# Mixer steps cut into pieces and placed between projections: a two-layer trunk on one core

## The chip, the core and the metric

One core of a Trainium2 chip runs the whole program. The metric is device microseconds of one execution, as the median of several runs. TensorE (PE) multiplies, VectorE (DVE) and ScalarE (ACT) work elementwise, GpSimd (POOL) does small elementwise work, SyncE (SP) issues the loads. Matrix products write PSUM, eight banks per partition, of which the kernel gives four to its pool a (projections), three to pool b (small steps) and one to sums.

## What is computed

Two layers, each a half-step SwiGLU feed-forward, four token mixers side by side with one input and one output projection, and a second feed-forward; 256 tokens, width 1024, everything in float32. Each section is normed and modulated by a conditioning vector.

```python
for l in range(DEPTH):
    cond = (c_act @ ada_w[l] + ada_b[l])[:, None, :]
    sh1, sc1, g1, sh2, sc2, g2, sh3, sc3, g3 = jnp.split(cond, N_MOD, axis=-1)
    h = modulate(rmsnorm(x, norm_g[l, 0]), sh1, sc1)
    x = x + 0.5 * g1 * swiglu(h, ffn1_w13[l], ffn1_w2[l])
    h = modulate(rmsnorm(x, norm_g[l, 1]), sh2, sc2)
    x = x + g2 * hybrid_mixer(h, ...)   # forgetting attention | mLSTM | retention | SSD, @ w_in before, @ w_out behind
    h = modulate(rmsnorm(x, norm_g[l, 2]), sh3, sc3)
    x = x + 0.5 * g3 * swiglu(h, ffn2_w13[l], ffn2_w2[l])
return rmsnorm(x, final_g)
```

In the mixers, the columns rq, rk (retention) are rotated, sx, sbc (SSD) and mq, mk (mLSTM) go through a causal convolution of four taps and a SiLU, mv, fv, rv are values, sz, mo, rg are gates, fq, fk are queries and keys of the forgetting attention.

## The kernel before

Activations lie feature by token (128 features by 256 tokens, eight tiles). Every float32 product is three products of a rounded type: each weight tile of 512 KB is loaded by SP into one of four buffers (raw), ACT rounds it (whi, L204), DVE subtracts (wlo, L205), and PE multiplies high by high, high by low and low by high (L222 to L224, or L767 to L769 for projections that come out token by feature). split() and wload() do this for all weights.

The conditioning vector is worked out beside everything else: each of its 128 rows that are not needed at the start is a 512 KB load (araw) and one multiply-and-sum on DVE (L263). Calls of background() in the feed-forward columns, the blocks of W2 and the projections start as many as the table BG says for the stage, in pairs (calls, sums); flush() makes up what a section needs.

A section's norm is put off: pre_begin and pre_tile scale the residual by the gain alone (uh, ul, with two extra columns for the shift), square it on ACT and add the squares on POOL (acc, L343). The first projections of a section run on these columns while the sum is finished: mm_two calls stat_end after six of eight feature tiles (L351 on PE, rs on ACT L372, a power on POOL L373), and later rows() (L378 on PE), which gives R, the row of norms. What was multiplied raw is then scaled by R and shifted. norm_h() makes the normed columns hh, hl for the rest (L407, L411, L412).

mixers_in walks through the list ORDER. A name with "p." projects (project), the others are steps that consume a projection or earlier steps; here every step is traced in one go. rq and rk are projected raw (proj_first), scaled in first_evac from PSUM; the others use h. Four PSUM banks hold projections. Steps use banks of pool b. Steps of the mixers proper: ssd (tables, scores, values), ret, mlstm, fox and foxb (softmax attention, front and back); ssdb, mo, rg, foxb make the four outputs y, which go through PE transposes and put_y into yh, yl. turns keeps outputs whose transposes are put off into W_out. W_out runs in two passes over all eight column tiles, with the outputs of fox and mLSTM first, then SSD and retention, holding the half-sums of eight tiles in four banks; in the second pass each tile is added to the residual (resid, L426) and taken up by pre_tile for the next section.

The order in which each engine gets its instructions is not the traced one. A scheduler takes instructions by a priority, which is the traced order (raised by HP within high_priority), as its own estimates say that their operands are ready; keep_in_program_order holds an instruction to its place on its engine. Each engine then takes its queue in order.

## Time and profile before

| | us |
|---|---|
| median of 3 runs | 1089.21 (1088.49 to 1089.78) |
| profiled execution, its own time | 1086.47 |
| its span, first to last instruction | 1084.7 |
| PE busy | 1055.8 (97%) |
| DVE busy | 856.0 (79%) |
| ACT busy | 535.9 (49%) |
| POOL busy | 68.8 (6%) |
| mean granted clock of PE | 0.993 |

The page counts an engine as busy while an instruction of it runs; products overlap on PE, so 283 ns is the time of one product from start to end, and one starts about every 0.12 us. Layer 0's mixers lie from 208 to 360 us, layer 1's from 740 to 884. The chain of work that ended last is PE for 76% of the span.

### The profile page before, as it was taken

How to read it: one execution, taken by the hardware profiler on the slowest of the kernel's cores; microseconds unless marked ns; L12 is line 12 of the kernel's file. 1: busy time of each engine (PE TensorE's matmuls, PEld its weight loads, DVE VectorE, ACT ScalarE, POOL GpSimd, SP SyncE). 2: the span in 40 equal slices, each digit the busy share in tenths (PEclk: the TensorE clock that was granted, in tenths of full speed). 3: DMA queues.
4: the chain of work that ended last, by engine and by line, in shares of the span. 5: the costliest groups of instructions: out<-in, count | busy, mean ns of one | idle time of the engine just before them, and what ended most of it. 6: DMA issues, size and time to landing. Idle time of an engine off the chain costs nothing.

```text
span 1084.7 us, 21679 instructions
## 1 busy us (share of the span) xinstructions
PE 1055.8 (97%) x8725; PEld 1039.9 (96%) x8725; DVE 856.0 (79%) x1505; ACT 535.9 (49%) x890; POOL 68.8 (6%) x87
## 2 busy tenths in 40 slices
PE   8999999889999999999999999999999999999997
PEld 6999999889899999999999999999999999999997
DVE  6899788879866999887679988767997689876551
ACT  4565434455445845434464543445545566554451
POOL 0000001200011300000100000012001130000010
PEclk9999999989999999999999999999999999999999
DMA  9889889947444679888657988865654366865541
GB/s 368 332 309 347 298 296 322 317 171 226 144 134 137 214 256 345 302 289 304 215 214 244 352 278 316 286 213 193 191 179 137 116 213 209 298 213 184 187 137 39
DMA packets 74022, 258.29 MB, mean 238 GB/s; under 512 B 10177, under 2 KB 12609, under 8 KB 73410
## 3 DMA queue, kind: packets, MB, share of 16 engines
q1 hardware_dynamic: 73634, 256.39, 68.5%
q8 instruction: 68, 1.11, 0.4%
q10 hardware_dynamic: 288, 0.52, 0.1%
q14 instruction: 32, 0.26, 0.1%
HBM read 255.83 MB, written 1.05 MB: 237 GB/s over the span
## 4 chain that ended last, share of the span: by engine, by line
PE 76%; DVE 8%; DMA 8%; issue 3%; ACT 3%; POOL 1%; SPq 0%; POOLq 0%; DVEq 0%; ACTq 0%
PE pa L222 22%; PE pa L223 22%; PE pa L224 22%; DMA araw<-in_ada_dram 3%; DVE wlo L205 2%; PE pa L769 2%; PE pa L767 2%; PE pa L768 1%; ACT whi L204 1%; DMA raw<-in_w2a_dram 1%; DVE araw L263 1%; PE pb L820 1%; DMA raw<-in_wfm_dram 1%; DVE ul L400 1%; DMA sh<-in_ada_dram 1%
## 5 line engine op out<-in xcount | busy, mean ns | idle before, releaser
L204 ACT ACTIVATE whi<-raw 128x1024 fp32r<-128x1024 f32 (+1 forms) x340 | 354.5, 1047 | 275.3 <-PE pa L223 79.4
L205 DVE TENSOR_TENSOR wlo<-raw,whi 128x1024 fp32r<-128x1024 f32 (+1 forms) x340 | 409.6, 1212 | 87.5 <-ACT whi L204 79.4
L222 PE MATMUL pa<-hh,whi 128*128 128x256 f32 x1424 | 403.2, 283 | 1.7 <-ACT whi L204 1.1
L223 PE MATMUL pa<-hl,whi 128*128 128x256 f32 x1424 | 403.4, 283 | 0.0
L224 PE MATMUL pa<-hh,wlo 128*128 128x256 f32 x1424 | 402.3, 283 | 0.5 <-DVE wlo L205 0.5
L222 PEld LDWEIGHTS pa<-hh,whi 128*128 128x128 f32 x1424 | 273.5, 192 | 3.6 <-ACT whi L204 2.3
L224 PEld LDWEIGHTS pa<-hh,wlo 128*128 128x128 f32 x1424 | 271.3, 191 | 1.2 <-DVE wlo L205 0.7
L223 PEld LDWEIGHTS pa<-hl,whi 128*128 128x128 f32 x1424 | 271.3, 191 | 0.5 <-issue 0.5
L263 DVE CUSTOM_DVE_ANT_0 araw<-araw,cact 128x1024 f32<-128x1024 f32 x128 | 158.1, 1235 | 48.1 <-DMA araw<-in_ada_dram 47.5
L224 PE MATMUL pa<-sh,wlo 128*128 128x256 f32 x660 | 184.3, 279 | 0.0
L222 PE MATMUL pa<-sh,whi 128*128 128x256 f32 x660 | 184.3, 279 | 0.0
L223 PE MATMUL pa<-sl,whi 128*128 128x256 f32 x660 | 184.3, 279 | 0.0
L222 PEld LDWEIGHTS pa<-sh,whi 128*128 128x128 f32 x660 | 125.1, 190 | 0.0
L224 PEld LDWEIGHTS pa<-sh,wlo 128*128 128x128 f32 x660 | 125.1, 190 | 0.0
L223 PEld LDWEIGHTS pa<-sl,whi 128*128 128x128 f32 x660 | 125.1, 189 | 0.0
L539 ACT ACTIVATE sh<-s 128x256 fp32r<-128x256 f32 x88 | 36.1, 411 | 116.0 <-DVE s L532 108.7
L343 POOL TENSOR_TENSOR acc<-acc,sq 128x256 f32<-128x256 f32 x40 | 35.8, 894 | 697.6 <-ACT sq L338 696.7
L223 PE MATMUL pa<-ul,whi 128*128 128x258 f32 x208 | 60.6, 291 | 2.5 <-DVE ul L400 2.5
L222 PE MATMUL pa<-uh,whi 128*128 128x258 f32 x208 | 61.2, 294 | 0.0
L767 PE MATMUL pa<-whi,hh 128*128 128x256 f32 (+1 forms) x192 | 57.0, 298 | 3.1 <-ACT hh L411 3.1
L224 PE MATMUL pa<-uh,wlo 128*128 128x258 f32 x208 | 60.0, 289 | 0.0
L769 PE MATMUL pa<-whi,hl 128*128 128x256 f32 (+1 forms) x192 | 56.0, 295 | 0.0
(276 smaller groups left out, 1379.6 us busy)
## 6 DMA issues: line engine op xcount, KB each, us to landing
araw<-in_ada_dram SPq DMA_DIRECT2D x128, 512.0 KB, 5.7
raw<-in_w13b_dram SPq DMA_DIRECT2D x88, 512.0 KB, 5.1
raw<-in_w13a_dram SPq DMA_DIRECT2D x76, 512.0 KB, 5.7
raw<-in_w2a_dram SPq DMA_DIRECT2D x44, 512.0 KB, 5.5
raw<-in_w2b_dram SPq DMA_DIRECT2D x44, 512.0 KB, 4.6
raw<-in_wfm_dram SPq DMA_DIRECT2D x32, 512.0 KB, 5.0
raw<-in_wtm_dram SPq DMA_DIRECT2D x24, 512.0 KB, 4.1
raw<-in_wo_dram SPq DMA_DIRECT2D x16, 512.0 KB, 4.7
```

Source lines behind the costliest of these rows:

```text
L204: act.activation(out=hi, in_=raw, func=AF.Copy)
L205: dve.tensor_tensor(out=lo, in0=raw, in1=hi.bitcast(F32), op=ALU.subtract)
L222: pe.matmul(o, lhsT=wh, rhs=xh, start=first, stop=False, **kw)
L223: pe.matmul(o, lhsT=wh, rhs=xl, start=False, stop=False, **kw)
L224: pe.matmul(o, lhsT=wl, rhs=xh, start=False, stop=last, **kw)
L263: dve.tensor_tensor_reduce(out=raw, in0=raw, in1=cact, scale=0.5, scalar=0.0, op0=ALU.mult, op1=ALU.add, accum_out=cond[l][:, i:i + 1])
L343: eng.tensor_tensor(out=s.acc, in0=s.acc, in1=sq, op=ALU.add)
L400: dve.scalar_tensor_tensor(out=s.ul[:, k, :T], in0=xT[:, k, :], scalar=s.G[:, k:k + 1], in1=s.uh[:, k, :T].bitcast(F32), op0=ALU.mult, op1 ...
L539: act.activation(out=sh[:, c, :], in_=s, func=AF.Copy)
L767: pe.matmul(os[t], lhsT=h[0][:, k, ts], rhs=wh[:, y, :], start=(k == 0), stop=False)
L768: pe.matmul(os[t], lhsT=h[0][:, k, ts], rhs=wl[:, y, :], start=False, stop=False)
L769: pe.matmul(os[t], lhsT=h[1][:, k, ts], rhs=wh[:, y, :], start=False, stop=(k == KT - 1))
```

## The change

- ORDER is written anew, and steps may be generators: a step runs to its next yield each time its name stands in ORDER (step()), so that a step's pieces lie between projections. There are nine yields per layer: two in ssd, one in ret, three in mlstm, two in fox (which takes in foxb), one in ssdb.
- sx is projected raw too, behind rq and rk. Raw projections are copied from PSUM by ACT (two copies each), and scaled by R later (rqe, rke, sxe).
- The convolutions of sbc, mq and mk read a copy in SBUF that ACT makes (copied) instead of PSUM.
- All POOL instructions are held in program order. The clearing of kz and bz becomes a step (clear) behind h; h is traced at high priority.
- The per-layer row of gate and norm parameters (row) is loaded in the first feed-forward of the layer.
- W_out takes six column tiles in two passes (SSD and retention first, then fox and mLSTM) in three banks, and the last two tiles in one pass each; the last piece of fox and the two put-off outputs lie among the first pass. The weights are laid out to match.
- BG: layer 0's first feed-forward starts 35 sums instead of 40, with 4 instead of 6 in its last three calls; layer 0's mixers 13 instead of 8, all in the last six projections; in the two feed-forwards between, more in the columns and fewer in W2.
- Two of the first four products of a feed-forward's raw columns go to banks of pool b. acc and R have one buffer instead of two.

```diff
-WO_GROUPS = ((0, 1), (3, 2))
-WO_TURNS = 2, 5
-WO_TILES = (0, 2, 4, 6, 1, 3, 5, 7)
+WO_GROUPS = ((3, 2), (0, 1))
+NP = 6
...
-BG = [((16, 15), (5, 13), (6, 12)), ((8, 0), (5, 8)), ((14, 14), (6, 0), (10, 18)), ((14, 14), (6, 0), (10, 18)),
-      ((8, 0), (5, 8)), ((14, 8),)]
+BG = [((16, 17), (1, 0), (7, 14), (3, 4)), ((8, 0), (6, 13)), ((2, 0), (13, 18), (5, 0), (10, 14)), ((2, 0), (13, 18), (5, 0), (10, 14)),
+      ((8, 0), (6, 8)), ((3, 0), (14, 8))]
...
-ORDER = """p.rq p.rk rq h p.mv gates rk p.sx mv sx p.sbc sbc p.rv p.mq p.mk rows rv ssd p.fk mk mq mlstm p.fq
- ret fq p.fv fk fv p.sz sz fox p.mo foxb mo p.rg ssdb rg""".split()
+ORDER = """p.rq p.rk h clear p.sx p.mv rqe rke rq gates rk p.sbc mv sxe sx sbc p.rv rv p.mq rows ssd ret p.mk ssd mq ret
+ p.sz ssd mk mlstm p.rg sz ssdb p.fk rg mlstm p.fq ssdb fk mlstm p.fv fq mlstm fox p.mo fv fox mo""".split()
+WO_STEPS = {1: "fox", 3: "turn", 5: "turn"}
+RAW = ("rq", "rk", "sx")
...
+        def __getattr__(self, name):
+            op = getattr(self.engine, name)
+            return lambda **kw: tc.keep_in_program_order(op(**kw))
+    pool = InOrder(nc.gpsimd)
...
-                og, oa = bank_a()[:, :TS], bank_a()[:, :TS]
+                og, oa = bank_a()[:, :TS], (bank_b() if c < 2 else bank_a())[:, :TS]
...
+            if i == 0 and c == NS + 4:
+                rows_of[l] = cp.tile([P, NC_ROW], F32, tag="row", name="row", bufs=1)
+                sp.dma_start(out=rows_of[l], in_=row_in[l][:NC_ROW].partition_broadcast(P))
...
-        for t in kz + [bz]:
-            pool.memset(t, 0.0)
-        row = mp.tile([P, NC_ROW], F32, name="row")
-        sp.dma_start(out=row, in_=row_in[l][:NC_ROW].partition_broadcast(P))
+        row = rows_of[l]
...
-            return os
-        def first_evac(os, R, tag):
-            r = mp.tile([P, 2, T], F32, tag=tag, name=tag, bufs=2 if tag == "rraw" else 1)
-            b = tp.tile([P, 2], F32, tag="fb", name="fb2")
+            r = mp.tile([P, 2, TS], F32, tag=dict(rq="rawrq", rk="ml", sx="rl")[name], name="raw" + name)
             for j in range(2):
-                act.activation(out=b[:, j:j + 1], in_=os[j][:, T:T + 1], func=AF.Copy)
-                dve.tensor_tensor(out=r[:, j, :], in0=os[j][:, :T], in1=R, op=ALU.mult)
-                act.activation(out=r[:, j, :], in_=r[:, j, :], func=AF.Identity, bias=b[:, j:j + 1])
+                act.activation(out=r[:, j, :], in_=os[j], func=AF.Copy)
             return r
+        def row_scaled(name):
+            r = v["o" + name]
+            dve.tensor_tensor(out=r[:, :, :T], in0=r[:, :, :T], in1=st.R.unsqueeze(1).to_broadcast([P, 2, T]), op=ALU.mult)
+            for j in range(2):
+                act.activation(out=r[:, j, :T], in_=r[:, j, :T], func=AF.Identity, bias=r[:, j, T:T + 1])
+            return r[:, :, :T]
...
+        def copied(o):
+            c = mp.tile([P, 2, T], F32, tag="cin", name="cin")
+            act.activation(out=c, in_=o, func=AF.Copy)
+            return c
...
+        def step(x):
+            if x not in running:
+                running[x] = parts[x]()
+            if running[x] is not None:
+                next(running[x], None)
...
+        banks = [bank_a() for _ in range(NB)]
         for g, grp in enumerate(WO_GROUPS):
...
+                tile(banks[n % NB][:, n // NB * T:(n // NB + 1) * T],
+                     [(wh[:, x, cs], wl[:, x, cs], grp[x // 2], x % 2) for x in range(4)], n, g == 0 and n < NB, g == 1, g == 1)
+        for k in range(NP, KT):
+            (wh, wl), = wload(wo[l][:, k * D:(k + 1) * D], 1, KT, P)
+            tile(bank_a()[:, :T], [(wh[:, x, :], wl[:, x, :], x // 2, x % 2) for x in range(KT)], k, True, True, True)
         return st
```

## Rows read from the trace of the kernel before

**Rows 1.** Busy times by stretch: stretch, its us, busy (instructions) per engine, clock, DMA, GB/s.

```profile
168.00:208.00 40.00, 40.00 (x347) 40.00 (x346) 36.25 (x50) 18.23 (x25) 5.44 (x5) 1.00 0.93 328
208.00:230.00 22.00, 16.75 (x111) 16.09 (x109) 13.12 (x21) 9.78 (x20) 5.24 (x8) 0.84 0.76 253
208.00:360.00 152.00, 142.17 (x1115) 138.10 (x1114) 118.53 (x267) 76.62 (x144) 17.16 (x21) 0.98 0.52 170
360.00:380.00 20.00, 18.53 (x151) 17.90 (x150) 19.91 (x37) 16.70 (x36) 5.32 (x5) 1.00 0.67 231
756.00:776.00 20.00, 18.45 (x133) 17.55 (x132) 18.09 (x43) 10.06 (x17) 1.43 (x3) 0.91 0.47 149
```

**Rows 2.** Order in time, PE, layer 0: start, us, instruction, [idle before <-releaser].

```profile
208.24 0.28 PE L222 MATMUL pa<-uh,whi 128*128 128x258 f32 x1
...
215.92 0.79 PE L351 MATMUL stat<-tab,acc 128*128 128x1 f32 x4 [3.20 <-POOL acc L343]
...
222.38 0.71 PE L378 MATMUL pb<-tab,rs 128*128 128x128 f32 x4 [2.05 <-POOL rs L373]
...
229.49 1.02 PE L1093 MATMUL pb<-rraw,tab 128*128 128x512 f32 x2
```

**Rows 3.** Order in time, PE, layer 1, the same instructions.

```profile
740.00 0.28 PE L222 MATMUL pa<-uh,whi 128*128 128x258 f32 x1
...
752.43 1.02 PE L1093 MATMUL pb<-rraw,tab 128*128 128x512 f32 x2
```

**Rows 4.** Order in time, DVE, layer 0, before the mixers' norm.

```profile
211.20 2.55 DVE L205 TENSOR_TENSOR wlo<-raw,whi 128x1024 fp32r<-128x1024 f32 x2 [0.24 <-ACT whi L204]
213.67 0.48 DVE L426 SCALAR_TENSOR_TENSOR xT<-pa,cond,xT 128x256 f32<-128x256 f32 x1
```

**Rows 5.** Order in time, ACT, layer 0, the same stretch.

```profile
211.44 1.06 ACT L204 ACTIVATE whi<-raw 128x1024 fp32r<-128x1024 f32 x1 [0.27 <-DMA raw<-in_wfm_dram]
...
221.18 0.20 ACT L912 ACTIVATE gea<-row 128x4 f32<-128x4 f32 x1 [6.18 <-DMA row<-in_row_dram]
221.29 0.24 ACT L372 ACTIVATE rs<-stat,epsc 128x2 f32<-128x2 f32 x1
```

**Rows 6.** Order in time, SP's queue of loads, layer 0.

```profile
214.18 0.42 SPq L720 DMA_DIRECT2D row<-in_row_dram  x1
```

**Rows 7.** Order in time, PE, layer 1: the wait for the normed columns.

```profile
758.49 0.39 PE L767 MATMUL pa<-whi,hh 128*128 128x272 f32 x1 [1.55 <-ACT hh L411]
```

**Rows 8.** PE's waits, 208 to 380 us, then 740 to 905: total, times, longest.

```profile
PE pb L970 <- DVE st L956: 1.5, 1, 1.5
PE pa L223 <- DVE ul L400: 1.2, 2, 0.7
PE pb L820 <- DVE sv L988: 1.0, 1, 1.0
PE pb L820 <- ACT pt L878: 0.5, 1, 0.5
...
PE pb L970 <- DVE st L956: 1.0, 1, 1.0
```

**Rows 9.** Order in time, layer 0: POOL's memset and addition, DVE's ul alone and beside the addition.

```profile
210.54 1.85 POOL L718 MEMSET kz<- 128x1024 f32 x2
...
354.48 2.19 POOL L343 TENSOR_TENSOR acc<-acc,sq 128x256 f32<-128x256 f32 x2 [13.42 <-ACT sq L338]
...
352.55 0.48 DVE L400 SCALAR_TENSOR_TENSOR ul<-xT,cond,uh 128x256 fp32r<-128x256 f32 x1
...
355.10 1.84 DVE L400 SCALAR_TENSOR_TENSOR ul<-xT,cond,uh 128x256 fp32r<-128x256 f32 x2
```

**Rows 10.** Groups of instructions, page and 208 to 355 us: count, busy us, mean ns, idle.

```profile
L205 DVE TENSOR_TENSOR wlo<-raw,whi 128x1024 fp32r<-128x1024 f32 (+1 forms) x340 | 409.6, 1212 | 87.5 <-ACT whi L204 79.4
...
L263 DVE CUSTOM_DVE_ANT_0 araw<-araw,cact 128x1024 f32<-128x1024 f32 x9 | 11.0, 1221 | 2.9 <-DMA araw<-in_ada_dram 2.9
...
L878 ACT COPY pt<-pb 128x512 f32<-128x512 f32 x4 | 2.1, 578 | 0.0
```

More of the change, by code (lines that the diff above doesn't have):

```diff
@@ L329, in stat_begin @@
         s.ps = ps_c.tile([P, 2], F32, tag="c", name="stat")
-        s.acc = tp.tile([P, T], F32, tag="acc", name="acc")
+        s.acc = tp.tile([P, T], F32, tag="acc", name="acc", bufs=1)
         s.sq = {}
@@ L957, in ssd_front @@
                 tabs.append((t0, t1))
+            yield
             for b in range(3):
@@ L1009, in ssd_back @@
                                          op0=ALU.mult, op1=ALU.mult)
-            turns.append((3, y))
+            yield
+            put_y(3, to_fm(y))
         def mlstm_front(mlf, arow, mq, mv):
@@ L1186, in e_ret @@
         def e_ret():
-            scaled(*ret_front(v["rq"], v["rv"]), "rl")
+            scaled(*(yield from ret_front(v["rq"], v["rv"])), "rl")
         def e_mlstm():
-            scaled(*mlstm_front(v["gl"][:, :, 4:8], v["arow"], v["mq"], v["mv"]), "ml")
+            scaled(*(yield from mlstm_front(v["gl"][:, :, 4:8], v["arow"], v["mq"], v["mv"])), "ml")
         def e_fq():
@@ L1208, in e_ssdb @@
         def e_ssdb():
-            ssd_back(v["xd"], v["z2"])
+            return ssd_back(v["xd"], v["z2"])
         def e_mo():
@@ L1235, in mixers_in, with tile @@
             else:
-                parts[x]()
+                step(x)
         flush(l, 5)
         st = done()
-        banks = []
+        def tile(o, ws, k, first, last, ended):
+            for z, (wh, wl, m, c) in enumerate(ws):
+                mm3(o, (wh, wl), (yh[:, m, c, :], yl[:, m, c, :]), first and z == 0, last and z == len(ws) - 1, skip_group_check=True)
+            if ended:
+                with tc.high_priority(HP):
+                    resid(l, 5, k, o)
+                    pre_tile(st, k)
+        NB = NP // 2
+        banks = [bank_a() for _ in range(NB)]
         for g, grp in enumerate(WO_GROUPS):
-            for n, k in enumerate(WO_TILES):
+            for n in range(NP):
                 if n % 2 == 0:
-                    (wh, wl), = wload(wo[l, g][:, n // 2 * D:(n // 2 + 1) * D], 1, 4, 2 * P)
-                if g == 0 and n < 4:
-                    banks.append(bank_a())
-                if g == 0 and n in WO_TURNS:
-                    m, y = turns.pop(0)
-                    put_y(m, to_fm(y))
-                o = banks[n % 4][:, n // 4 * T:(n // 4 + 1) * T]
-                cs = slice(n % 2 * P, (n % 2 + 1) * P)
-                for x in range(4):
-                    m, c = grp[x // 2], x % 2
-                    mm3(o, (wh[:, x, cs], wl[:, x, cs]), (yh[:, m, c, :], yl[:, m, c, :]),
-                        g == 0 and n < 4 and x == 0, g == 1 and x == 3, skip_group_check=True)
-                if g == 1:
-                    with tc.high_priority(HP):
-                        resid(l, 5, k, o)
-                        pre_tile(st, k)
+                    (wh, wl), = wload(wo[l][:, (g * NB + n // 2) * D:(g * NB + n // 2 + 1) * D], 1, 4, 2 * P)
+                if g == 0 and n in WO_STEPS:
+                    step(WO_STEPS[n])
+                cs = slice(n % 2 * P, (n % 2 + 1) * P)
+                tile(banks[n % NB][:, n // NB * T:(n // NB + 1) * T],
[3 more added lines that the diff above has]
+            tile(bank_a()[:, :T], [(wh[:, x, :], wl[:, x, :], x // 2, x % 2) for x in range(KT)], k, True, True, True)
         return st
```

107 lines of the change are left out of this document (62 added, 45 removed).

## The prediction

> **What bounds the kernel now.** I read the table of stretches first, the busy times of each engine between fixed times [rows 1]. TensorE (PE) is the bound: in the stretch before the first mixers it is busy for all of 40.00 us, with the DMA engines at 0.93. It stands still at few places, and almost all of them lie in and just behind the two mixer stages (208 to 360 us in layer 0, 740 to 884 us in layer 1), where PE is busy 142.17 of 152.00 us in layer 0. VectorE (DVE) is the next engine there, 118.53 of 152.00 us; ScalarE (ACT) has 76.62. So a change of the mixers is worth what it takes out of PE's waits, and it may add work on ACT and some on DVE.
>
> The order of PE's instructions in time says where the waits are. The first 96 products of each mixer stage (rq and rk, on the columns u) are the same in both layers. In layer 0 they begin at 208.24 and the rotary product behind them starts at 229.49, 21.25 us later [rows 2]; in layer 1 it is 740.00 to 752.43, 12.43 us [rows 3]. The 8.8 us of difference are two waits (3.20 us for the sum of squares, 2.05 us for the power on POOL) and the clock: the stretch 208 to 230 has a mean granted clock of 0.84, thus some 7 us at the lower level of 1.2 GHz, each time after a wait [rows 1, 2].
>
> Why those two waits? DVE's list shows the first: the last column tile of the residual (L426) runs at 213.67, 5.4 us after PE went on to u, because it stands in DVE's queue behind two weight splits that ran at 211.20 [rows 4]; the high part of the second of them started only at 211.44, when the DMA of its weights had landed [rows 5]. ACT's list shows the second: the instruction for the statistics (rs, L372) stands behind gea (L912), which stood 6.18 us for the DMA of row [rows 5], which SP issued only at 214.18 [rows 6]. In layer 1 the background sums end early and neither matters.
>
> **The change part by part.** I make the sum against the profiled execution (span 1084.7, its time 1086.47) and carry the difference to the median of the runs, 1089.21, which is 2.7 above it; I assume that all three move alike.
>
> (A) Hand-over into layer 0's mixers. The row load moves into the feed-forward stage, some hundred microseconds before its use, so gea cannot hold rs any more: the 2.05 us wait and the half clock behind it go. The first feed-forward stage gets 35 conditioning sums instead of 40, and 4 instead of 6 in its last three calls of background(); each is a 512 KB load on DMA engines that were at 0.93, and 1.2 us of DVE [rows 1, 10]. So the split weights of rq and rk come earlier and the last residual need not stand behind them. Bounds: layer 1 shows the state without both waits, 8.8 us; the rs wait alone with half of the lower clock is 2.05 + 1.7 = 3.7 us. I take 7.5, near the upper end, since layer 1 runs the same instructions. Row's 400 KB and the sums come back elsewhere: row beside a stage in which PE had no wait, the sums as five more in layer 0's mixers, in its last six projections, where the DMA engines stood at 0.52 over the stage [rows 1]. The DVE time is 5 x 1.2 = 6.1 us.
>
> (B) The normed columns h. Now the third projection (mv) needs them and PE stands 1.55 us in layer 1 and as long in layer 0 for hh [rows 7]; in layer 1 the lower clock follows (0.91 over 756 to 776 [rows 1], so 3.6 us of it, of which nearly half is lost, 1.6). Together 4.7. Now sx comes third and raw: its 48 products, half of the 96 that took 12.43 us [rows 3], so some 6 us, lie ahead of the first need of h, the four banks of rq and rk are emptied by ACT copies at once, and the scaling of rq and rk moves behind mv. That is more than the wait. But DVE has the splits of sx and mv (four at 1.21 [rows 10]) beside 16 norm steps, so I take 3.5 (bounds 0 and 4.7).
>
> The clearing of kz and bz moves to the same place, beside that norm chain. In the trace two of its memsets take 1.85 us on POOL [rows 9], while DVE's two splits at 211.20 take 2.55 us [rows 4], 1.27 each against a mean of 1.21 [rows 10]. So I cost it at 0.1 us per layer, that is, at nothing. It is not so for additions: the ul step of DVE takes 0.48 alone and 0.92 (1.84 for two) beside POOL's additions into acc [rows 9]. The Trainium skill (GPSIMD Engine Reference, Key points) says that GpSimd shares its SBUF interfaces with VectorE and contends with instructions of two SBUF inputs, which the norm steps are; by that rule the memsets would stretch the norm chain by as much as they last. The trace agrees for the additions and not for the memsets.
>
> (C) Steps in pieces. PE's waits inside the mixers are 1.5 us for the SSD tables, 1.0 for its values, 0.5 for the transposed probabilities in layer 0, and 1.0 and 0.5 for the first and the last again in layer 1 [rows 8]; together 4.5. Nine cuts per layer (yield) now put a projection, or another step, between a piece's last PE instruction and the next piece that needs DVE's or ACT's answer; a projection is some 6 us of PE. I take 3.0. The same cuts can make waits where there are none: a piece waits if DVE's queue holds splits, conv taps and conditioning sums ahead of what it needs. What a seam costs no row shows; the nearest are the waits just named, 0.5 to 1.5 us each. Bounds for 18 cuts: 0 (their gain is the 4.5 above, and no more), and 18 x 1.0 = 18. I take 2.0 in all, near the lower end, since of the many step starts of the kernel before only these few wait.
>
> (D) Into the second feed-forward stage. From 360 to 380 PE stands 1.47 us and DVE is busy 19.91 of 20.00 [rows 1]; the waits are for ul, 1.2 us in two, in both layers [rows 8]. DVE does two instructions per finished column tile (0.48, and 0.92 beside POOL [rows 9]) and half a split, 2.0 us, while PE makes a tile of 12 products of 0.12 in 1.4 (96 products take 12.43 with the two small steps among them [rows 3]). Before, eight tiles end in this way and DVE falls 4.8 us behind; now six do (3.6), and the last two have 24 products, 2.8 us, against 0.48 + 0.92 + 1.21 = 2.6. So DVE enters the next stage about 1.5 us less late. Of 2 x 1.47 I take 1.6 (bounds 0 and 2.9).
>
> The other edits I cost at nothing: three ACT copies of convolution inputs per layer at 0.58 each (the like copy from PSUM, [rows 10]) and six raw copies run on an engine that is half idle, and give the banks back sooner; the taps then read SBUF, and no row says that this is faster. The two extra columns of sx are 2 of 258. Pinning POOL's order costs nothing while its queue is short. If ACT's idle half were gone, the copies would be some 5 us per layer of ACT, still beside PE.
>
> Sum: -7.5 - 3.5 - 3.0 - 1.6 + 2.0 = -13.6. Span 1084.7 to 1071.1, its time 1086.47 to 1072.9, median 1089.21 to 1075.6.
>
> **The rivals.** *Seams (the other side).* The scheduler places pieces by its own estimates and PE takes its queue in order, so a piece that is too early holds the projection behind it. For: DVE is already at 118.53 of 152 and gets 6.1 us more in a shorter stage, so answers come late. Against: only three such waits per layer now. If each of 18 cuts waits the mean of the three rows, 1.0 us, then 18 is added, C's gain does not come, and the rest (-12.6) stays: 1089.2 + 5.4 = 1094.6. It decides from a mean of 0.7 us per cut, where the gain is gone.
>
> *DVE becomes the bound of layer 0's late mixers.* 118.5 + 6.1 = 125 us of work in a stage of about 140. At the one place where DVE is full (19.91 of 20) PE loses 1.47 of 20 us [rows 1]; over the last six projections with their steps, about 60 us, that is 4.4. Time 1075.6 + 4.4 = 1080.
>
> *The change does not do what it says.* The written order is only a priority; the trace of before shows single products of mv and sx mixed, so the scheduler already puts projections between steps. Then B, C and D hardly move, and only A stays: 1089.2 - 7.5 = 1081.7.
>
> *Memsets against the norm chain.* If they took DVE's time as the additions do, 1.85 us a layer would be added to B and its gain be halved or lost: 1075.6 + 3.5 = 1079. The row on splits beside memsets [rows 4] speaks against it, so 0.04.
> The rule of the Trainium skill (GPSIMD Engine Reference, Key points) that bears on this rival is told under B.
>
> **How the numbers follow.** Forecast (1068 to 1080) 0.58; DVE bound 0.10; only A 0.10; memsets 0.04; seams 0.18, of which 0.06 near the point where they eat the gain and 0.12 beyond. About 0.2% (2.2 us) is what a measurement can tell here. Faster 0.82, same 0.06, slower 0.12. The range of 8 in 10 runs from 1066 to 1088. Its lower end is all bounds of A to D without a cost at the seams, 20.9 less, thus 1068.3, and 2 more because the listed waits are idle time alone and PE's pace just around each loses some tenths besides. Its upper end takes in the three rivals on the fast side and half of those seams that eat the gain. Left out are the slower seams (0.12) and some 0.08 at both ends.
>
> **What would show it.** A: rq's first product to the first step behind the raw products without a gap over 1 us and a granted clock of 1.00 in layer 0's hand-over; no ACT wait on row. B: no PE wait for hh of more than 0.5 us. C: the sum of PE's waits for st, sv and pt below 1.5 us in both layers; new waits, if any, named for DVE and ACT tiles of pieces behind a cut. D: PE's idle time in the first 20 us of the feed-forward stage below 0.8. I am wrong if mixers are not shorter by at least 8 us in layer 0, or if PE's idle time only moves to new names.

## The result and the profile after

The changed kernel takes 1074.73 us, the median of four executions (1072.46 to 1076.33), beside 1088.85 us for the kernel before: a ratio of 0.987 with a 95% interval of 0.983 to 0.992. The forecast was 1075.6 us, faster; the interval lies below 1, so it is faster beyond the noise. The executions of one kernel differ mostly by the clock that they are granted: of 31 of the kernel before one took 1082.90 us at a mean clock of 0.997 and one 1096.69 at 0.983. The mean over these 31 is 0.991, that over the four of the changed kernel 0.998; by an estimate from these means (0.9% of 1089 less 0.2% of 1075) some 7 to 8 of the 14 us lie in the clock. The profiled execution of after took 1072.46 us (span 1070.7), 14.0 us below that of before (1086.47, span 1084.7).

TensorE's first product on u and on the gated columns marks the borders of the stages, so the two traces can be laid side by side:

| stage (us) | before | after | difference |
|---|---|---|---|
| mixers, layer 0 (first u product to the next stage's first) | 152.25 | 142.23 | -10.0 |
| mixers, layer 1 | 143.99 | 141.72 | -2.3 |
| second feed-forward, columns, layer 0 | 129.04 | 128.62 | -0.4 |
| second feed-forward, columns, layer 1 | 129.13 | 128.68 | -0.45 |
| first feed-forward, columns, layer 1 | 127.71 | 126.90 | -0.8 |
| all other stages | | | under 0.1 |

The table of stretches of after, to be read against [rows 1] (stretch, its us, busy us and instructions of PE, PEld, DVE, ACT and POOL, clock, DMA, GB/s):

```profile
208.00:230.00 22.00, 22.00 (x184) 22.00 (x184) 15.67 (x28) 14.36 (x29) 3.72 (x5) 1.00 0.59 188
208.00:350.00 142.00, 138.47 (x1115) 134.80 (x1115) 120.36 (x271) 79.45 (x150) 17.47 (x22) 1.00 0.56 183
350.00:370.00 20.00, 18.53 (x154) 18.26 (x154) 19.17 (x35) 15.81 (x32) 3.08 (x3) 1.00 0.77 258
```

In the 22 us of the hand-over PE is now busy for all of 22.00 at a clock of 1.00, where it had 16.75 at 0.84. In layer 0's mixers its idle time fell from 9.83 to 3.53 us, in layer 1's only from 3.41 to 3.16. The lower clock, which cost 3.4 and 1.7 us in these two stages before, shows in neither after. In the first 20 us of the second feed-forward it is still 1.47 us, to the hundredth.

The hand-over itself, and what keeps it short: PE's first product on u and the first that needs normed columns (PE), DVE's conditioning sum, splits and norm step, then ACT's rs:

```profile
208.19 0.28 PE L238 MATMUL pa<-uh,whi 128*128 128x258 f32 x1
226.37 0.29 PE L784 MATMUL pa<-whi,hh 128*128 128x272 f32 x1
215.30 1.22 DVE L279 CUSTOM_DVE_ANT_0 araw<-araw,cact 128x1024 f32<-128x1024 f32 x1 [5.36 <-DMA araw<-in_ada_dram]
216.45 2.35 DVE L221 TENSOR_TENSOR wlo<-raw,whi 128x1024 fp32r<-128x1024 f32 x2
218.72 0.48 DVE L423 SCALAR_TENSOR_TENSOR xr<-xT,cond,R 128x256 f32<-128x256 f32 x1
213.05 0.26 ACT L388 ACTIVATE rs<-stat,epsc 128x2 f32<-128x2 f32 x1 [3.32 <-PE stat L367]
```

144 products take 18.18 us without a gap, 0.126 each, close to layer 1's pace before (12.43 for 96 with the first steps behind them, 0.129, [rows 3]). ACT waits for the statistics and not for row; no split stands between the residual and u on DVE, which was idle for 5.36 us ahead of 215.30. The norm's steps end as the third raw projection does, and mv starts without a wait.

PE's waits of after from 200 to 1000 us (what waited, for what, total us, times, longest), against [rows 8]:

```profile
PE pb L394 <- POOL rs L105: 2.8, 2, 1.5
PE pb L1136 <- DVE rows L862: 2.4, 2, 1.7
PE pb L868 <- DVE fm L1097: 1.5, 1, 1.5
PE pb L817 <- DVE ry L1247: 0.8, 1, 0.8
PE pb L875 <- DVE yl L828: 0.5, 1, 0.5
PE pb L898 <- ACT pt L895: 0.5, 2, 0.2
PE pb L894 <- ACT pp L1102: 0.4, 1, 0.4
PE pa L239 <- DVE yl L828: 0.4, 1, 0.4
```

The waits for st, sv and ul are gone, that for pt is 0.5 us in all. New names stand in their place: the statistics of the second feed-forward (rs), the row sums (rows), fox's row maxima (fm), the gated output of retention (ry). The second of them, on DVE in layer 0:

```profile
254.57 0.87 DVE L973 TENSOR_SCALAR st<-tab,lah 128x128 fp32r<-128x128 f32 x4
255.35 1.22 DVE L221 TENSOR_TENSOR wlo<-raw,whi 128x1024 fp32r<-128x1024 f32 x1
256.61 0.55 DVE L862 TENSOR_TENSOR rows<-pb,rt 8x384 fp32r<-8x384 f32 x1
```

Retention's scores need a bank of pool b, and the row sums still hold it. DVE takes the row sums (rows, L862) only behind the last SSD tables and a split, though ACT's part of them had run at 253.47.

### The profile page after: what moved, and what is told of

The parts are those of the page before. It is cut to its first block, busy times and chain, and to the rows that moved or that the text cites. A ratio compares the mean times of both kernels' runs of the same rounds, so it can differ in the third digit from the quotient of the medians.

```text
span 1070.7 us, 21683 instructions
## 1 busy us (share of the span) xinstructions
PE 1049.5 (98%) x8725; PEld 1035.1 (97%) x8725; DVE 857.2 (80%) x1503; ACT 544.6 (51%) x904; POOL 65.4 (6%) x87
## 3 DMA queue, kind: packets, MB, share of 16 engines
HBM read 255.83 MB, written 1.05 MB: 240 GB/s over the span
## 5 line engine op out<-in xcount | busy, mean ns | idle before, releaser
L238 PE MATMUL pa<-hh,whi 128*128 128x256 f32 x1392 | 395.4, 284 | 0.8 <-ACT whi L220 0.8
L240 PE MATMUL pa<-hh,wlo 128*128 128x256 f32 x1392 | 393.1, 282 | 0.5 <-DVE wlo L221 0.5
L239 PE MATMUL pa<-hl,whi 128*128 128x256 f32 x1392 | 392.9, 282 | 0.0
L238 PEld LDWEIGHTS pa<-hh,whi 128*128 128x128 f32 x1392 | 267.0, 192 | 3.2 <-issue 1.8
L240 PEld LDWEIGHTS pa<-hh,wlo 128*128 128x128 f32 x1392 | 265.1, 190 | 0.7 <-DVE wlo L221 0.7
L239 PEld LDWEIGHTS pa<-hl,whi 128*128 128x128 f32 x1392 | 265.0, 190 | 0.6 <-issue 0.5
L238 PE MATMUL pa<-uh,whi 128*128 128x258 f32 x192 | 55.2, 288 | 0.0
L785 PE MATMUL pa<-wlo,hh 128*128 128x256 f32 (+1 forms) x192 | 54.5, 284 | 0.0
L239 PE MATMUL pa<-ul,whi 128*128 128x258 f32 x192 | 54.3, 283 | 0.0
```

Source lines behind the costliest of these rows:

```text
L238: pe.matmul(o, lhsT=wh, rhs=xh, start=first, stop=False, **kw)
L239: pe.matmul(o, lhsT=wh, rhs=xl, start=False, stop=False, **kw)
L240: pe.matmul(o, lhsT=wl, rhs=xh, start=False, stop=last, **kw)
L785: pe.matmul(os[t], lhsT=h[0][:, k, ts], rhs=wl[:, y, :], start=False, stop=False)
```

## The experiments

Times of one kernel differ by 2 to 15 us between executions here, so each edit is read first from the stages of its trace; the medians and ratios stand beside them. But a trace is one execution, and a fall of the clock in it need not be in the others: b_row's trace is the shortest of ten, those of a_rowsfox and a_last are the longest of their executions. Where a stage differs by the clock and not by PE's idle time, the text says so. Stages in us (mixers of layers 0 and 1, columns of the second feed-forwards), with the profiled time and the median:

| kernel | mixers 0 | mixers 1 | columns 0 | columns 1 | profiled | median | ratio to before, interval |
|---|---|---|---|---|---|---|---|
| before | 152.25 | 143.99 | 129.04 | 129.13 | 1086.47 | 1088.85 | |
| after | 142.23 | 141.72 | 128.62 | 128.68 | 1072.46 | 1074.73 | 0.987 (0.983 to 0.992) |
| b_row | 144.81 | 143.70 | 129.34 | 129.17 | 1079.62 | 1084.90 | 0.998 (0.994 to 1.002) |
| b_bg | 146.11 | 143.26 | 129.03 | 129.13 | 1079.66 | 1079.90 | 0.993 (0.990 to 0.996) |
| b_row_bg | 144.47 | 145.50 | 129.09 | 129.19 | 1080.97 | 1083.68 | 0.996 (0.994 to 0.998) |
| a_sx_h | 149.42 | 144.18 | 127.46 | 128.70 | 1083.82 | 1079.22 | 0.993 (0.990 to 0.995) |
| a_whole | 144.14 | 143.85 | 127.41 | 127.56 | 1075.79 | 1078.51 | 0.993 (0.990 to 0.996) |
| a_np8 | 140.51 | 141.92 | 130.17 | 130.22 | 1078.93 | 1078.77 | 0.991 (0.988 to 0.994) |
| a_pool_free | 141.25 | 141.81 | 128.54 | 127.53 | 1072.16 | 1072.66 | 0.987 (0.981 to 0.993) |
| a_nocopy | 143.93 | 143.84 | 128.70 | 127.53 | 1076.70 | 1077.70 | 0.990 (0.986 to 0.993) |
| a_rowsfox | 145.40 | 140.75 | 127.44 | 128.68 | 1078.40 | 1073.16 | 0.988 (0.983 to 0.992) |
| a_best | 141.18 | 140.92 | 130.95 | 130.21 | 1083.09 | 1087.52 | 1.000 (0.997 to 1.003) |
| a_clear | 142.84 | 148.27 | 127.40 | 128.66 | 1080.33 | 1079.56 | 0.993 (0.989 to 0.996) |
| a_last | 148.84 | 140.18 | 128.58 | 128.68 | 1079.96 | 1076.30 | 0.990 (0.986 to 0.993) |

### Step A, from the side of the kernel before: row early, rates of the background work, both

**b_row**

```diff
+            if i == 0 and c == NS + 4:
+                rows_of[l] = cp.tile([P, NC_ROW], F32, tag="row", name="row", bufs=1)
+                sp.dma_start(out=rows_of[l], in_=row_in[l][:NC_ROW].partition_broadcast(P))
...
-        row = mp.tile([P, NC_ROW], F32, name="row")
-        sp.dma_start(out=row, in_=row_in[l][:NC_ROW].partition_broadcast(P))
+        row = rows_of[l]
```

(For the space, acc and R have one buffer, as in the change.)

> The kernel before, with one part of the change alone: the row of constants is loaded in the first feed-forward into a tile that stays, not at the start of the mixers (acc and R have one buffer instead of two, for the space). Theory (step A of the prediction): ACT's gea no longer waits for the row's DMA, so that the reciprocal root rs behind it comes earlier: layer 0's hand-over, 21.25 us from the first u product to the rotary product in the kernel before, loses the 2.05 us wait and part of the half clock, 17 to 19.3 us; the 3.2 us wait for the statistics stays. The whole: 1084 to 1087 us. Rival (the residual behind the splits decides alone): hand-over within 0.5 us of 21.25, the whole 1088 to 1090.

**b_bg**

```diff
-BG = [((16, 15), (5, 13), (6, 12)), ((8, 0), (5, 8)), ...
+BG = [((16, 17), (1, 0), (7, 14), (3, 4)), ((8, 0), (6, 13)), ...
```

> The kernel before, with the new rates for the background work in the first layer's first feed-forward and mixers alone. Theory (step A): the splits and conditioning sums that stand ahead of the last residual on DVE move, so that the 3.2 us wait for the statistics at layer 0's hand-over goes; the wait behind the row's DMA takes its place at least in part, as rs now wants ACT earlier while the row lands when it did: hand-over 17 to 20 us instead of 21.25, the whole 1085 to 1088. Rival (the rates don't decide what stands ahead of the residual): 21 us or more, the whole 1088 to 1091.

**b_row_bg**: both edits.

> The kernel before with both parts, the early row and the new rates. Theory (step A): both causes gone, hand-over 12.4 to 13.5 us as in layer 1, the whole 1079 to 1082, and the gain is more than the sum of the two alone, as either one holds the other's place. Rival (the hand-over of the changed kernel is short for its new order of projections and its POOL order): hand-over 16 us or more, the whole 1083 or more.

The first u product to the rotary product: 21.25 us before, 14.73 in b_row, 12.40 in b_bg, 12.41 in b_row_bg. PE's wait that was left in b_row, its hand-over stretch, and then in b_bg the residual, ACT's gea with rs behind it, and SP's issue of row:

```profile
215.03 0.61 PE L352 MATMUL stat<-tab,acc 128*128 128x1 f32 x4 [2.04 <-POOL acc L344]
208.00:230.00 22.00, 18.41 (x141) 17.14 (x140) 17.61 (x32) 12.25 (x27) 5.26 (x8) 1.00 0.72 234
```

```profile
208.41 0.48 DVE L426 SCALAR_TENSOR_TENSOR xT<-pa,cond,xT 128x256 f32<-128x256 f32 x1 [2.52 <-PE pa L224]
213.82 0.20 ACT L912 ACTIVATE gea<-row 128x4 f32<-128x4 f32 x1 [4.08 <-PE stat L351]
213.93 0.24 ACT L372 ACTIVATE rs<-stat,epsc 128x2 f32<-128x2 f32 x1
208.40 0.33 SPq L720 DMA_DIRECT2D row<-in_row_dram  x1
```

Both hand-overs are shorter than was expected, but only the rates show a gain beyond the trace. In b_row the wait for the statistics stayed (2.04 us of 3.20), the other was gone, and with it the whole fall of the clock: 1.00 over the stretch, not 0.84. Of the 6.5 us saved 3.4 are the clock. This was the shortest of ten executions, though, with a mean clock of 0.997. Over all ten the mean clock is 0.991, as it is over the 31 of the kernel before, and the ratio, 0.998 (0.994 to 1.002), shows no gain. What the early row is worth alone is not shown.

In b_bg both waits went (mean clock 0.996 over ten executions, 0.4 to 1.0% faster). The residual ran at 208.41 and not at 213.67 [rows 4], since DVE stood free for it; and SP issued row at 208.40 and not at 214.18 [rows 6], with fewer background loads ahead of it in its queue, so gea was done as rs came. The two causes were one: too many conditioning sums in the last calls of the stage before. Both rivals fall in the traces, and so does my view that either cause would hold the other's place.

Together the edits give the full hand-over and 7.8 us of the 10.0 in layer 0's mixers. By the times the gain of both is 0.2 to 0.6%, not more than that of the rates alone, and the median, 1083.68, is above the 1079 to 1082 that was expected. In layer 1 this trace shows 1.5 us more than before; that is the clock (0.72 over 796 to 808 us), as PE's idle time there is the same (3.45 us for 3.41).

### Step B: two raw projections in the changed kernel

```diff
-RAW = ("rq", "rk", "sx")
+RAW = ("rq", "rk")
```

(sxe leaves ORDER, and sx's convolution reads an ACT copy.)

> The changed kernel, with two raw projections instead of three: sx is projected from the normed columns h, as before, and copied by ACT ahead of its convolution like sbc. Theory (step B): in the changed kernel the norm chain ends about when the third raw projection does; without it PE waits for h again: 1.5 to 4 us in each layer, the mixers 143.7 to 146.5 us in layer 0 (142.23 in the changed kernel) and 143.2 to 145.7 in layer 1 (141.72), the whole 1078 to 1082. Rival (the norm's high priority alone hides the chain): no wait for hh over 0.5 us, both mixers within 0.7 us of the changed kernel's, the whole 1073 to 1076.

PE's waits of a_sx_h in layer 0's hand-over (208 to 240 us), and its stretch from mv's first products on:

```profile
PE pa L785 <- DVE wlo L221: 1.0, 1, 1.0
PE pa L238 <- ACT hh L427: 0.3, 1, 0.3
...
221.00:230.00 9.00, 7.58 (x45) 6.89 (x44) 8.59 (x18) 5.13 (x11) 0.00 (x0) 0.81 0.54 178
```

The wait is back, most of it under another name: mv's low split (wlo) now stands among the last steps of the norm on DVE, 1.0 us, with 0.5 for hh and hl. The same stretch of after has PE busy for all of 9.00 at 1.00. The idle time is 1.4 us, and 0.81 over 9 us means 3.4 us at 1.2 GHz, which loses 1.7: 3.1 us. In layer 1 the waits are 1.2 us and the clock stays at 1.00. Layer 1's mixers lengthen by 2.5 us, as expected; layer 0's by 7.2, more than expected, because 3.5 us of a wait for fm, where after has none in layer 0, and another 1.7 us for the clock (0.83 over 320 to 330 us) come on top further on. The rival (priority alone hides the chain) falls.

### Step C: steps run whole in the changed kernel

```diff
             if running[x] is not None:
                 next(running[x], None)
+                while x in WHOLE and next(running[x], 0) is None:
+                    pass
+WHOLE = "ssd", "ret", "mlstm", "ssdb"
```

> The changed kernel, with the steps ssd, ret, mlstm and ssdb run whole where ORDER names them first; only fox and the turns are still cut. Theory (step C of the prediction, with what the trace after shows): the cuts took away waits for st, sv and pt (4.5 us in both layers together) and brought others (PE for the bank of the row sums 1.7 and 0.7, the rest at fm and ry, that don't hang on these cuts): uncut, 4.5 come back and 2.4 go, both mixers together 283.95 + 2 = 286 us (1 to 4 more than now), the whole 1075 to 1079. Rival 1 (the seams cost more than they save): mixers shorter by 1 us or more in sum, the whole 1072 or less. Rival 2 (the cuts carry most of the gain): mixers longer by 8 us or more in sum, the whole 1081 or more.

PE's waits of a_whole, 200 to 1000 us:

```profile
PE pb L818 <- DVE sy L1028: 3.7, 2, 2.0
PE pb L869 <- DVE cum L1038: 1.9, 2, 1.0
PE pa L239 <- DVE xT L443: 1.5, 2, 1.2
PE pb L989 <- DVE st L974: 1.4, 2, 0.7
PE pb L395 <- POOL rs L106: 0.5, 2, 0.3
```

Both mixers together are 4.0 us longer, the upper end of what was expected, and the wait for rows is gone, as expected. But what came back is not what the cuts had removed. Only st is an old name, at 1.4 of its 2.5 us; the others are sy (3.7 us: the SSD output is normed right ahead of its transposes), cum and a tile of the residual (xT). Of the 4.0 us 1.8 are PE's idle time and 1.7 a fall of the clock in layer 1 (0.83 over 820 to 830 us). 2.3 us are given back in the columns of the second feed-forwards, where the wait for rs falls from 2.8 to 0.5. In this order of projections the cuts are worth some 2 to 4 us. Against the kernel before, which had other waits in another order, the mixers show no gain by them (see C below).

### Step D: the output projection over eight tiles in two passes

```diff
-NP = 6
+NP = 8
```

> The changed kernel, with the output projection again in two passes over all eight tiles (six in two passes and two at full depth in the change). Theory (step D): the last two tiles of the two-pass form end close together, so the residual, uh, ul and the squares of both stand between the last product and the statistics; PE waits for ul in the second feed-forward again, 0.7 to 1.2 us in each layer, and the wait for rs (1.5 us in each) moves later by as much or takes it up: first 20 us of each second feed-forward together 0.5 to 2.5 us longer, the whole 0.5 to 3 us more. Rival (what stands ahead of rs on ACT, a split of the next column's weights, decides alone): no difference over 0.3 us in either layer.

PE's wait of a_np8 at the start of layer 0's second feed-forward (340 to 372 us), and the first 20 us of that stage:

```profile
PE stat L367 <- POOL acc L105: 1.6, 1, 1.6
349.00:369.00 20.00, 18.42 (x142) 18.21 (x141) 18.65 (x33) 15.37 (x34) 5.31 (x5) 0.91 0.70 227
```

The columns on u, from their first product to the start of their last, take 21.41 and 21.48 us instead of 19.87 and 19.93: 3.1 us more in both layers, where 0.5 to 2.5 was expected. But it is not PE's idle time that grew: it is 1.58 us in these 20, where after and before have 1.47. It is the clock, 0.91 over the 20 us in both layers, which loses 1.8 us; after has 1.00 there. The wait is for the sum of squares (acc), one step behind ul, and after has one of the same size for rs. So a_np8 does not show that the two tiles at full depth take idle time out, as D said: one wait stands for another, and in this execution the clock fell behind one of them and not behind the other. And layer 0's mixers are 1.7 us shorter with eight, so there the form moves time. Its second products of layer 0 took 65.86 us against 61.38; that is the wait described under a_best.

### What was costed at nothing: POOL's order and ACT's copies

```diff
-            return lambda **kw: tc.keep_in_program_order(op(**kw))
+            return lambda **kw: op(**kw)
```

> The changed kernel, with POOL's operations ordered by the scheduler as before and not by the program. Theory (costed at nothing in the prediction): POOL is busy for under a tenth of the mixers, and what it does it does when its input is there: the stages within 0.5 us, the whole within 0.2%. Rival: the program order keeps the memsets of the clear step away from rs and the sums of squares at the hand-over, without it layer 0's hand-over (18.18 us) is 1 us longer or more; or it holds up a pow of the head norms, and without it the mixers are 1 us shorter or more.

The whole does not move: span 1070.4 against 1070.7, median 1072.66, hand-over 18.27 against 18.18. Single stages move by up to 1.15 us in either direction, more than the 0.5 expected (layer 0's mixers 0.98 shorter, the first feed-forward of layer 1 1.05 longer, the second 1.15 shorter), and cancel.

```diff
         def copied(o):
-            c = mp.tile([P, 2, T], F32, tag="cin", name="cin")
-            act.activation(out=c, in_=o, func=AF.Copy)
-            return c
+            return o
```

> The changed kernel, with the convolutions of sbc, mq and mk reading PSUM as before, without ACT's copies (three of 0.58 us in each layer). Theory (costed at nothing): the copies lie beside PE's work; what they give is that a bank of pool a comes free some 2 to 4 us earlier, and it waits for none at present: mixers within 0.7 us in each layer, the whole within 0.2%. Rival 1 (DVE bound: VectorE's convolution products read SBUF faster than PSUM): DVE's convolution group gets longer by over 10% and the mixers by 1 to 3 us in each layer. Rival 2 (the bank): PE waits for a bank of pool a for 1 us or more.

Two of PE's waits of a_nocopy in layer 0's mixers, and DVE's groups of one tap reading PSUM and reading the copy (count, busy us, mean ns):

```profile
PE pa L238 <- DVE g L724: 1.0, 1, 1.0
PE pa L784 <- DVE cva L717: 0.8, 1, 0.8
```

```profile
L717 DVE SCALAR_TENSOR_TENSOR cva<-pa,col,cva 128x253 f32<-128x253 f32 x6 | 2.9, 478 | 0.1
L717 DVE SCALAR_TENSOR_TENSOR cva<-cin,col,cva 128x253 f32<-128x253 f32 x6 | 2.8, 478 | 0.0
```

The mixers are 1.7 and 2.1 us longer. The taps take 478 ns from either memory, so the first rival falls, and the second holds: a projection waits for a bank of pool a until DVE has done its last tap (cva, 0.8) or its gating (g, 1.0), 1.8 us in each layer. Other waits move as well (in layer 0 rows falls by 1.4 us, and fm waits 1.5 where after has none; in layer 1 ry waits 1.1), so the bank's share of the 1.7 and 2.1 us can't be told apart from theirs. The copies were not free to leave out; by the medians they are worth some 3 us.

### The norm chain beside POOL's work

```diff
         def e_clear():
-            for t in kz + [bz]:
-                pool.memset(ap=t, constant=0.0)
+            for x in range(5 if l == 0 else 1):
+                for t in kz + [bz]:
+                    pool.memset(ap=t, constant=0.0)
+            for x in range(4 if l == 1 else 0):
+                pool.tensor_tensor(out=kz[x % 2], in0=kz[x % 2], in1=kz[x % 2], op=ALU.add)
```

> The changed kernel, with more work for POOL beside VectorE's norm chain (xr and hl, 0.48 us each in both layers now, the memsets end before it): in layer 0 the clearing of kz and bz five times over (2.3 us becomes some 11.7, from 214 to 226 us), in layer 1 four additions of 128x1024 behind the clearing (some 11 us from 737 to 748 us). Theory (from the rows of before: splits beside memsets 1.27 us against 1.21 alone, ul beside additions 0.92 against 0.48): memsets leave xr and hl at 0.48 to 0.52 and layer 0's hand-over at 18.2 to 18.7 us; additions make them 0.8 to 0.95 and layer 1's hand-over 3 us longer or more. Rival (the shared interface is taken by any work of POOL): xr and hl go to 0.7 or more in layer 0 too, and its hand-over is 2 us longer or more.

Layer 0's norm steps under memsets (xr's durations: least, median, most), then in layer 1 POOL's four additions and DVE's first four xr beside them:

```profile
L423 DVE SCALAR_TENSOR_TENSOR xr<-xT,cond,R x8: 474/478/480, 218.9 to 223.7; 128x256 f32<-128x256 f32 x8
220.82 1.86 POOL L105 MEMSET kz<- 128x1024 f32 x2
738.15 8.81 POOL L105 TENSOR_TENSOR kz<-kz 128x1024 f32<-128x1024 f32 x4
741.07 6.57 DVE L423 SCALAR_TENSOR_TENSOR xr<-xT,cond,R 128x256 f32<-128x256 f32 x4
```

Layer 0: no step is longer than 0.48 us, and the hand-over stays at 18.18. Layer 1: four xr take 6.57 us where after has 1.67, the longest alone 2.11 us, so three of them waited 1.63 us each for an addition (3 x 1.63 = 4.9 = 6.57 - 1.67), not each for half as much as was expected; PE then waits 3.6 us for wlo, the clock falls (0.66 over 749 to 759 us, which loses 3.4), and the mixers are 6.6 us longer. So additions stop DVE's two-input steps while they run, and memsets cost them nothing. The Trainium skill (SBUF — State Buffer, Who interferes with whom) draws the line in the same place: a VectorE instruction with two SBUF inputs contends with a GpSimd one that reads SBUF, not with one that only writes it, and the loser is blocked for the whole instruction. The trace agrees with both halves.

### Attempts to do better

The waits that are left point to orders, and three edits tried to mend them.

**a_rowsfox**: the last SSD tables are ordered behind the row sums (L862) on DVE, and fox's first piece ahead of mlstm's last, in both layers.

```diff
- ... p.fv fq mlstm fox p.mo fv fox mo
+ ... p.fv fq fox mlstm p.mo fv fox mo
+            rowsop[:] = [nc.cur_bb.bb.instructions[-1].name]
+                    tc.add_manual_dep(nc.cur_bb.bb.instructions[-1], rowsop[0], ...)
```

> The changed kernel, with two orders mended: the last eight tables of ssd (those of 128 columns) stand behind the row sums on VectorE, and fox's first piece comes ahead of mlstm's last one. Theory (the waits that the change brought in at its seams are VectorE's order, nothing else): PE's wait for the bank of the row sums (1.7 us in layer 0, 0.7 in layer 1) and its wait for fm (1.5 in layer 1) go, other waits take up to half of it: both mixers together 1.9 to 3.9 us shorter than 283.95, the whole some 1071 to 1073 on the profile's scale of 1072.5 for the changed kernel. Rival (VectorE is full there, and the tables or mlstm's tail are late next): the sum of both mixers within 1 us of 283.95, the waits only at other names.

Its waits in layer 0's mixers, and two stretches of them:

```profile
PE pb L838 <- DVE fm L1101: 1.5, 1, 1.5
PE pb L1140 <- DVE rows L863: 0.8, 1, 0.8
310.00:320.00 10.00, 8.50 (x56) 8.09 (x55) 5.29 (x21) 1.88 (x6) 0.00 (x0) 0.85 0.60 211
320.00:330.00 10.00, 10.00 (x74) 10.00 (x73) 6.86 (x16) 7.28 (x21) 1.64 (x1) 0.80 0.32 97
```

In layer 0 the wait for rows fell from 1.7 to 0.8, but fm waits 1.5 us where it had not, the clock falls to 0.85 and 0.80 over 20 us (3.0 and 4.0 us at 1.2 GHz, half of which is lost, 3.5 us), and the mixers are 3.2 us longer. PE's idle time in them is 3.80 us for 3.53, so what they lose is the clock, in the longest of four executions; the other three took 1070.82 to 1073.73 us. In layer 1 they are 1.0 us shorter. Neither the theory nor its rival holds for both layers.

**a_best**: the same, and in the second feed-forward the split of the second column's second half is ordered behind rs on ACT.

```diff
+        if behind[0] and behind[1] == 2:
+            tc.add_manual_dep(getattr(op, "ins", op), behind[0], ...)
```

> The same two orders, and in the second feed-forwards ACT forms the mean of squares (rs) ahead of the split of the second column's second half instead of behind it. Theory (the 1.5 us wait for rs at the start of each second feed-forward is ACT's order): both second feed-forwards' column stages 128.62 and 128.68 shorter by 0.8 to 1.5 us each, the whole 3 to 6 us below the changed kernel. Rival 1 (POOL's power beside VectorE's splits, 1.6 us instead of 0.7, is what PE waits for): stages shorter by under 0.5 us. Rival 2 (the split that now waits is late for the second column): a new wait for whi or wlo of 0.7 us or more, stages not shorter.

```profile
PE pa L246 <- DVE wlo L227: 1.9, 1, 1.9
PE pb L402 <- POOL rs L105: 1.4, 1, 1.4
355.55 1.06 ACT L221 ACTIVATE whi<-raw 128x1024 fp32r<-128x1024 f32 x1 [2.23 <-DMA raw<-in_w13b_dram]
356.51 0.24 ACT L395 ACTIVATE rs<-stat,epsc 128x2 f32<-128x2 f32 x1
```

(PE's waits in layer 0, 350 to 380 us, and ACT in order.) The second rival came true, and the wait for rs stayed as well: the scheduler now set another split ahead of it, one that waited 2.23 us for its DMA, and the later splits are late for their columns (wlo, 1.9 us). The columns are 2.3 and 1.5 us longer, and the median of twelve executions, 1087.52 us, is 13 above the changed kernel's. A residual of layer 0's second products also waited 4.7 us for DVE, which stood idle for conditioning loads ahead of it (0.91, 1.46 and 1.63 us among them); that stage took 68.94 us against 61.38. The same wait shows in a_np8, a_rowsfox and a_last with 1.4 to 2.3 us, not in after. As the median of a_rowsfox (1073.16) lies 5 us below its profiled execution, it need not be in every execution; why those loads are late is open.

**a_last**: fox ahead of mlstm's end in layer 1 alone, and rg cut ahead of its turn into yh.

> The changed kernel, with rg cut ahead of its turn into yh (the second piece after ssdb's last, one projection later), and in layer 1 alone fox's first piece ahead of mlstm's last. Theory (the waits for ry, 0.8 us in layer 0, and for fm, 1.5 us in layer 1, are a matter of where the step stands, and no clock falls if no new wait passes 1.5 us): layer 0's mixers 141.3 to 142.2 us (142.23 in the changed kernel), layer 1's 140 to 141 (141.72), the whole 1 to 3 us below the changed kernel's 1072.5. Rival (each seam that is moved opens another of its size, as it did with fox moved in both layers, where layer 0's mixers took 145.4): the sum of both mixers within 0.7 us of 283.95 or above it.

Layer 1's mixers took 140.18 us, 1.5 less: the one edit that did what it should, with fm's wait at 1.0 and no fall of the clock. In layer 0 the cut of rg removed the wait for ry (0.8) and made others, for pt and for the bank of a turn into yh, where rg's and ssdb's now stand together; a wait for fm is there too, and the clock falls to 0.83 here and once more from 254 to 264 us, which loses 3.4 us of the 6.6 that the stage is longer:

```profile
PE pb L868 <- DVE fm L1097: 1.9, 1, 1.9
PE pb L898 <- DVE yl L828: 1.7, 1, 1.7
...
304.00:314.00 10.00, 6.87 (x44) 6.46 (x44) 6.25 (x10) 5.25 (x8) 0.00 (x0) 0.83 0.77 266
```

So no version was found that is clearly below the changed kernel: the intervals of a_pool_free and a_rowsfox overlap with its own. Fox's order in layer 1 without the cut of rg was not measured alone.

## Why the prediction was right, and where its steps were not

**The whole.** -13.6 us was forecast, -14.0 came in the profiled executions and -14.1 between the medians. The mixers of layer 0 are 10.0 us shorter (at least 8 was named). Of the 12.3 us in both mixers 6.5 are PE's idle time and 5.1 the falls of the clock that the kernel before had there (3.4 and 1.7), which A and B had counted in. But the sum is -8.8 - 4.7 + 1.2 - 0.9 by the four parts and -0.8 that no part held, against -7.5 - 3.5 - 1.0 - 1.6: no term came at its size, and that it meets the time within 0.4 us is luck.

**A**, -7.5 forecast, -8.8 measured at the hand-over, the whole difference between the layers and its upper bound; in b_row_bg, which has A alone, layer 0's mixers keep 7.8 of it. All signs named came: no gap, a clock of 1.00, no ACT wait on row. The mechanism had one fault: I took the row load for the remedy of the wait behind gea and the rates for that of the residual. By b_bg the rates alone do both, because SP's queue held row up for the same loads; what the row load adds is not shown. Of the 8.8 us the two waits are 5.25 and the clock 3.4, as the prediction had it.

**B**, -3.5 forecast, -4.7 by the waits of before that are gone (1.5 in layer 0; 1.6 and the clock's 1.6 in layer 1); a_sx_h shows 3.1 and 1.2 in the hand-overs, 4.3 in all. The step that made me take less than the full 4.7, the splits of sx and mv beside the norm steps on DVE, did not come true: DVE ran mv's splits at 223.87 and 226.26, among the last steps of the norm, and PE did not wait for either.

**C**, -3.0 with +2.0 for the seams forecast; what is left of the mixers' differences when A and B are taken out is +1.2 (-12.3 in both, against -8.8 and -4.7). So the step that C gains 1.0 net failed. Its sign named for right came: st, sv and pt together wait 0.5 us. But so did a sign named for wrong, as this idle time only moved to new names: 6.0 us stand in place of 4.5. And the seams were mis-sized in kind: not many small waits, but four of 0.8 to 1.7 us and some of 0.5 or less, the large ones each at a step whose answer stands in DVE's queue behind something else (rows behind the tables, fm behind mlstm's norm, ry behind the SSD output). 6.0 over 18 cuts is 0.33 each, half of the 0.7 from which the rival decides.

**D**, -1.6 forecast, -0.9 measured, and not as told. PE's idle time in the first 20 us is 1.47 as before, so the sign named for right (below 0.8) did not come. ul no longer waits, but rs does, with 1.47 and 1.36 us: here too the idle time only moved to a new name. Over the whole columns of both layers it is 2.83 us for 2.93, so 0.1 of the 0.9 is idle time; for the rest, in which PE is busy for less time, no run shows the cause. What I missed is what is late next: rs on ACT stood behind a split that waited for its DMA (0.43 us), and then POOL's power took 1.60 us. Before, the power took 1.48 us there too, behind the waits for ul. What the stage would give without the wait for rs, a_whole shows: its columns, where that wait is 0.5 us in two, are 1.6 us shorter than before in each layer.

**At nothing.** POOL's order: nothing. ACT's copies: wrong, the mixers are 1.7 and 2.1 us longer without them, and PE waits 1.8 us a layer for banks of pool a that DVE's taps and gating hold. No row of before showed that, since there the convolutions stood elsewhere in the order. Beyond the sum, 0.8 us came in the first feed-forward of layer 1, where before PE waited 0.6 us for the first scaled column (gR) and after waits for nothing. a_pool_free and a_nocopy are 1.0 and 1.3 us longer there, with waits of 0.8 and 1.0 us for rs. None of the edits touches this stage alone, and no run shows which part of the change took the wait out.

**The rivals.** Seams: its mechanism is there, its price half of what it needed. DVE's bound: DVE is at 120.36 of 142.00 and PE at 138.47, so it is an order on DVE, not its total, that PE waits for. Only A: refuted by b_row_bg, whose ratio (0.994 to 0.998) lies above the changed kernel's (0.983 to 0.992), and by the traces of a_sx_h, a_whole and a_nocopy, each of which loses 3.8 us or more in the mixers. Memsets: refuted by a_clear, where they cover the whole chain; the row of before that spoke against it was thin, as the memsets lay beside 1.2 of the 2.55 us of splits.

## What to carry to other kernels

When two waits stand close together, look for one cause ahead of both in the queues (here a few background loads too many), and price the fall of the clock behind them as part of it: here it was 3.4 of 8.8 us. Cutting a step into pieces moves a wait to wherever the piece's answer is queued, so look up for each new piece what stands ahead of it on the in-order engine, and cut only where that queue is short. An edit that frees a bank or an engine early can be worth more than it looks even where nothing waits for it yet, as soon as the order of the work around it changes.

## What was not expected of the hardware

POOL's power on two elements takes 0.70 or 0.71 us where DVE is idle (213.39), and 1.60 where it starts just behind a split's start: then it ends 0.56 us after the split, as if it began only then. In order, POOL and DVE of after, then of a_whole, where the power starts late in a split (358.31 to 359.52) and again ends 0.56 us after it:

```profile
213.39 0.71 POOL L105 TENSOR_TENSOR rs<-rs,half 128x2 f32<-128x2 f32 x1 [2.78 <-ACT rs L388]
357.45 1.60 POOL L105 TENSOR_TENSOR rs<-rs,half 128x2 f32<-128x2 f32 x1 [2.74 <-ACT fb L568]
354.92 3.57 DVE L221 TENSOR_TENSOR wlo<-raw,whi 128x1024 fp32r<-128x1024 f32 x3
359.31 0.77 POOL L106 TENSOR_TENSOR rs<-rs,half 128x2 f32<-128x2 f32 x1 [2.35 <-ACT fb L569]
```

It looks like a_clear's effect from the other side: there POOL's addition held DVE, here DVE's split would hold POOL. No run moves a split away from the power alone.

The clock did not fall behind every wait. PE stood 1.66 us of 10 in layer 0 of after at a clock of 1.00, and 2.04 us in b_row at 1.00, but behind 1.5 us in a_rowsfox it fell to 0.85 and 0.80, and behind 1.6 us in a_np8 to 0.91, where after stood 1.47 us at 1.00:

```profile
250.00:260.00 10.00, 8.34 (x61) 7.82 (x60) 9.89 (x28) 4.24 (x7) 0.00 (x0) 1.00 0.48 154
```

What decides between them these rows don't tell; the 1.5 us of a_last's expectation is no bound that they bear out.
